# Rotary embedding on one half of each head: tile 2 loaded as 11 and 5 rows in place of 8 and 8

## The chip, the cores and the metric

The kernel runs on one core of a Trainium2 chip. The metric is the device time of one execution in microseconds. Before the change its median is 161.76 us over 3 runs (161.6 to 161.9).

## What is computed

The input `x` has the shape (16, 512, 16, 64) in float32: batch, sequence, heads, and 64 values per head. The tables `cos` and `sin` have the shape (512, 32). The first 32 values of each head are rotated; the other 32 are copied.

```
x1, x2 = x[..., :32], x[..., 32:]
c, s = cos[None, :, None, :], sin[None, :, None, :]
first  = x1[..., :16] * c[..., :16] - x1[..., 16:] * s[..., :16]
second = x1[..., :16] * s[..., :16] + x1[..., 16:] * c[..., :16]
out = concatenate([first, second, x2], axis=-1)
```

## The kernel before

Seen as one long array, `x` is cut into T = 4 tiles of 128 partitions. A partition holds K = 16 rows of the sequence, and a row is 16 heads of 64 values, 4 KB. A whole tile is 64 KB per partition, 8.4 MB in all. The tiles pass through SBUF in a ring of NS = 3 places (`ring`), tile t in place t modulo 3. Tiles are rotated in their place and stored from there, so tile 3 takes the place of tile 0 and can be loaded only when tile 0 has been stored.

`load` (L55) and `store` (L58) each issue one DMA over a stretch of rows, all loads and most stores from the queue of SP. SP works through its orders one by one: an order that waits holds up all orders behind it. Only the store of tile 2 is issued from GpSimd. SP's orders are, in this sequence: tile 0, tile 1, the upper 8 rows of tile 2 (`load(2, KC, K)`, KC = 8), the store of tile 0 (waits for VectorE), the lower 8 rows of tile 2, tile 3 (waits for the store of tile 0), the store of tile 1, the store of tile 3.

VectorE first builds the tables in all partitions (L61 to L83) out of two small loads that GpSimd issues (L63, L64). Then `rotate` does the work, four instructions per call over a stretch of rows of a tile: a product with sin into `b_t`, which lies in PSUM (L96), a product with cos in place (L97), a subtraction (L98) and an addition (L101). Tiles 0, 1 and 3 are rotated in two parts of 8 rows. Tile 2 is rotated as rows 8 to 15, rows 0 to 4 and rows 5 to 7; the border is KM = 5. The part with 5 rows is called `near`: a dependency written by hand (`tc.add_manual_dep`) lets the store of tile 1 wait until its last addition.

Of the kernel before, what the change touches and what calls it, by code (L numbers as in the profile page):

```python
# [1 line left out]

# [4 lines left out]


@with_exitstack
def kernel(  # L10
    ctx: ExitStack,
    tc: tile.TileContext,
    x: bass.AP,
    cos: bass.AP,
    sin: bass.AP,
    out: bass.AP,
):
    nc = tc.nc
    fp32 = mybir.dt.float32
    P = 128  # L20
    B, S, H, D = x.shape
    Q = D // 4
    HF = D // 2

    K = 16
    T = B * S // (P * K)
    PB = S // K
    REP = P // PB  # L30
    R = H * D
    NS = 3
    KC = K // 2
    KM = 5

    xf = x.rearrange("b s h d -> (b s h d)").rearrange("(t p f) -> t p f", t=T, p=P)
    of = out.rearrange("b s h d -> (b s h d)").rearrange("(t p f) -> t p f", t=T, p=P)
    cosf = cos.rearrange("(p k) j -> p (k j)", k=K)
    sinf = sin.rearrange("(p k) j -> p (k j)", k=K)

    const_pool = ctx.enter_context(tc.tile_pool(name="const", bufs=1))
    b_pool = ctx.enter_context(tc.tile_pool(name="bp", bufs=1, space=bass.MemoryType.PSUM))


    ring = const_pool.tile([P, NS, K, H, D], fp32)
    stage = const_pool.tile([P, 2, K, HF], fp32)
    spun = const_pool.tile([P, 2 * K, Q], fp32)
    packed = const_pool.tile([PB, 2 * K, Q], fp32)
    table = const_pool.tile([P, 2, K, 2, Q], fp32)

    def rows(t, lo, hi):
        return ring[:, t % NS, lo:hi].rearrange("p k h d -> p (k h d)")

    def load(t, lo=0, hi=K):
        return nc.sync.dma_start(out=rows(t, lo, hi), in_=xf[t, :, lo * R : hi * R])  # L55

    def store(t, lo=0, hi=K, queue=nc.sync):
        return queue.dma_start(out=of[t, :, lo * R : hi * R], in_=rows(t, lo, hi))  # L58


    nc.vector.memset(stage[:, :, :, 0:Q], 0.0)  # L61
    spread = stage.rearrange("(j b) t k i -> j b t (k i)", b=REP)
    nc.gpsimd.dma_start(out=spread[:, 0, 0], in_=cosf)  # L63
    nc.gpsimd.dma_start(out=spread[:, 0, 1], in_=sinf)  # L64
    load(0)
    load(1)
    load(2, KC, K)

    PQ = PB // REP
    nc.vector.stream_shuffle(  # L73
        out=spun[:],
        in_=stage.rearrange("p t k j -> p (t k) j")[:, :, 0:Q],
        mask=[j % PQ * REP for j in range(PB)],
    )
    for q in reversed(range(REP)):
        n = PQ * (q + 1)
        nc.vector.tensor_copy(out=packed[0:n], in_=spun[q * PB : q * PB + n])  # L80

    for r in range(REP):
        nc.vector.tensor_copy(  # L83
            out=table[r * PB : (r + 1) * PB].rearrange("p t k c j -> p (t k) c j"),
            in_=packed.unsqueeze(2).to_broadcast((PB, 2 * K, 2, Q)),
        )
    C = table[:, 0].rearrange("p k c j -> p k (c j)")
    Sn = table[:, 1].rearrange("p k c j -> p k (c j)")

    def rotate(t, lo, hi):  # L90
        x1 = ring[:, t % NS, lo:hi, :, 0:HF]
        c = C[:, lo:hi].unsqueeze(2).to_broadcast((P, hi - lo, H, HF))
        s = Sn[:, lo:hi].unsqueeze(2).to_broadcast((P, hi - lo, H, HF))
        b_full = b_pool.tile([P, KC, H, HF], fp32, name="b_t")
        b_t = b_full[:, 0 : hi - lo]
        nc.vector.tensor_mul(out=b_t, in0=x1, in1=s)  # L96
        nc.vector.tensor_mul(out=x1, in0=x1, in1=c)  # L97
        nc.vector.tensor_sub(  # L98
            out=x1[:, :, :, 0:Q], in0=x1[:, :, :, 0:Q], in1=b_t[:, :, :, Q:HF]
        )  # L100
        return nc.vector.tensor_add(  # L101
            out=x1[:, :, :, Q:HF], in0=x1[:, :, :, Q:HF], in1=b_t[:, :, :, 0:Q]
        )

    rotate(0, 0, KC)
    rotate(0, KC, K)
    store(0)
    load(2, 0, KC)
    load(3)
    rotate(1, 0, KC)  # L110
    rotate(1, KC, K)
    behind_loads = store(1)
    rotate(2, KC, K)
    near = rotate(2, 0, KM)
    rotate(2, KM, KC)
    store(2, queue=nc.gpsimd)

    tc.add_manual_dep(
        behind_loads.ins,
        near.ins.name,  # L120
        mybir.DependencyInfo(mybir.DependencyClass.Sync, mybir.DependencyReason.DATA),
        reason="the store follows the loads at the DMA engines",
    )
    rotate(3, 0, KC)
    rotate(3, KC, K)
    store(3)


# [1 line left out]
_INS = ['x', 'cos', 'sin']  # L130
_OUTS = [((16, 512, 16, 64), 'float32')]


# [23 lines left out]
```

## Time and profile before

| | |
|---|---|
| median of 3 runs | 161.76 us (161.6 to 161.9) |
| span of the profiled execution | 159.5 us |
| median less span | 2.3 us |
| VectorE busy | 112.9 us, 71% |
| DMA queues, share of 16 engines | 85.7% (SP's) and 12.4% (GpSimd's) |
| moved | 67.24 MB, 422 GB/s over the span |
| one rotation of 8 rows | 4.43 + 4.42 + 2.29 + 2.28 us on VectorE |
| store of tile 0 | issued at 49.92 us, lands after 21.8 us |
| load of tile 3 | issued at 71.72 us, lands after 29.0 us |
| last store | issued at 131.24 us, lands after 27.4 us |

Times in the trace are counted from the start of the span. A DMA order has two times: the issue on the queue's sequencer, some 0.4 us long, and the landing, when the last of the 16 DMA engines has reported. In between, the engines move packets, one for each partition and order, up to 64 KB long, eight of them per engine and order. The digits of the page's DMA line count a packet in the slice where it starts. The span begins and ends with the program's first and last instruction on the core; the run's time also holds what lies around it.

### The profile page before, as it was taken

To read this page: it belongs to the slowest core of one execution; us is meant where nothing else is said; L and a number is where in the kernel's file an instruction comes from. 1 tells how busy PE (TensorE), PEld (TensorE's weight loads), DVE (VectorE), ACT (ScalarE), POOL (GpSimd) and SP (SyncE) were. 2 spreads that over 40 slices of the span, in tenths; PEclk is the share of its full clock that TensorE was granted. 3 is DMA by queue.
4 is the path that set the end of the run, shared out by engine and by line. 5 is a ranking of instruction groups with operands and counts; after the bars stand their busy time and mean duration, and the time that the engine had idled before them with its cause. 6 is when DMAs were issued, how large, how long until landed. Compare 5 with 4: busy or idle time off the path is not lost.

```text
span 159.5 us, 115 instructions
## 1 busy us (share of the span) xinstructions
DVE 112.9 (71%) x47; POOL 1.9 (1%) x7
## 2 busy tenths in 40 slices
DVE  1000959999999999999999999999999990000000
POOL 3000000000000000000000000010000000000000
DMA  7969979799699699699996996996996997999966
GB/s 263 542 263 542 444 345 526 345 444 526 271 493 551 279 510 526 263 394 411 510 526 263 526 526 263 526 526 263 526 526 263 526 460 329 526 394 394 526 263 263
DMA packets 1360, 67.24 MB, mean 422 GB/s; under 512 B 176, under 2 KB 176, under 8 KB 208
## 3 DMA queue, kind: packets, MB, share of 16 engines
q1 hardware_dynamic: 1152, 58.72, 85.7%
q0 software_dynamic: 208, 8.52, 12.4%
HBM read 33.69 MB, written 33.55 MB: 422 GB/s over the span
## 4 chain that ended last, share of the span: by engine, by line
DVE 61%; DMA 14%; issue 5%; DVEq 1%
DVE b_t L96 22%; DVE ring L97 22%; DMA ring<-in_x_dram 14%; DVE ring L101 10%; DVE ring L98 7%; DVEq L152 1%; DVEq L96 0%
## 5 line engine op out<-in xcount | busy, mean ns | idle before, releaser
L96 DVE TENSOR_TENSOR b_t<-ring,table 128x4096 f32<-128x4096 f32 (+2 forms) x9 | 35.6, 3959 | 2.1 <-DMA ring<-in_x_dram 1.8
L97 DVE TENSOR_TENSOR ring<-ring,table 128x4096 f32<-128x4096 f32 (+2 forms) x9 | 35.5, 3950 | 0.3
L98 DVE TENSOR_TENSOR ring<-ring,b_t 128x2048 f32<-128x2048 f32 (+2 forms) x9 | 18.4, 2049 | 0.3
L101 DVE TENSOR_TENSOR ring<-ring,b_t 128x2048 f32<-128x2048 f32 (+2 forms) x9 | 18.4, 2043 | 0.0
L73 DVE LOAD_MASK_SELECT spun<-stage x1 | 0.0, 14 | 14.4 <-DMA stage<-in_sin_dram 14.4
L83 DVE COPY table<-packed 32x1024 f32<-32x1024 f32 x4 | 2.7, 684 | 0.1
L58 POOL DMA_DIRECT2D out_dram<-ring x1 | 0.6, 562 | 101.7 <-DVE ring L101 101.7
L80 DVE COPY packed<-spun 32x512 f32<-32x512 f32 (+3 forms) x4 | 1.7, 416 | 0.1
L61 DVE MEMSET stage<- 128x512 f32 x1 | 0.5, 485 | 0.9 <-PEq L141 0.9
L73 DVE STREAM_SHUFFLE spun<-stage 128x512 f32<-128x512 f32 x1 | 0.7, 721 | 0.0
L63 POOL DMA_DIRECT2D stage<-in_cos_dram x1 | 0.6, 644 | 1.3 <-DVE stage L61 1.3
L64 POOL DMA_DIRECT2D stage<-in_sin_dram x1 | 0.5, 535 | 0.0
L141 POOL MEMSET const-bfloat16-1.0<- 128x1 bf16 x1 | 0.1, 102 | 0.0
L141 POOL MEMSET const-float32-0.0<- 128x1 f32 x1 | 0.1, 99 | 0.2 <-issue 0.2
L141 POOL MEMSET const-float32-1.0<- 128x1 f32 x1 | 0.1, 99 | 0.0
L141 POOL MEMSET const-uint8-127<- 128x1 uint8 x1 | 0.1, 99 | 0.0
## 6 DMA issues: line engine op xcount, KB each, us to landing
ring<-in_x_dram SPq DMA_DIRECT2D x2, 4096.0 KB, 40.7
stage<-in_cos_dram POOLq DMA_DIRECT2D x1, 64.0 KB, 9.0
stage<-in_sin_dram POOLq DMA_DIRECT2D x1, 64.0 KB, 13.3
ring<-in_x_dram SPq DMA_DIRECT2D x3, 29.0
out_dram<-ring SPq DMA_DIRECT2D x3, 27.4
out_dram<-ring POOLq DMA_DIRECT2D x1, 39.5
```

The costliest lines, as they stand in the source:

```text
L58: return queue.dma_start(out=of[t, :, lo * R : hi * R], in_=rows(t, lo, hi))
L61: nc.vector.memset(stage[:, :, :, 0:Q], 0.0)
L63: nc.gpsimd.dma_start(out=spread[:, 0, 0], in_=cosf)
L64: nc.gpsimd.dma_start(out=spread[:, 0, 1], in_=sinf)
L73: nc.vector.stream_shuffle(out=spun[:], in_=stage.rearrange("p t k j -> p (t k) j")[:, :, 0:Q], mask=[j % PQ * REP for j in range(PB)],)
L80: nc.vector.tensor_copy(out=packed[0:n], in_=spun[q * PB : q * PB + n])
L83: nc.vector.tensor_copy(out=table[r * PB : (r + 1) * PB].rearrange("p t k c j -> p (t k) c j"), in_=packed.unsqueeze(2).to_broadcast((PB, ...
L96: nc.vector.tensor_mul(out=b_t, in0=x1, in1=s)
L97: nc.vector.tensor_mul(out=x1, in0=x1, in1=c)
L98: nc.vector.tensor_sub(out=x1[:, :, :, 0:Q], in0=x1[:, :, :, 0:Q], in1=b_t[:, :, :, Q:HF])
L101: return nc.vector.tensor_add(out=x1[:, :, :, Q:HF], in0=x1[:, :, :, Q:HF], in1=b_t[:, :, :, 0:Q])
L152: with _tile.TileContext(nc) as tc:
```

## The change

The rows of tile 2 are divided otherwise over its two loads. Ahead of the store of tile 0 SP now orders rows 5 to 15 (11 rows), and behind it rows 0 to 4 (5 rows). VectorE's parts of tile 2 become rows 8 to 15, rows 3 to 7 and rows 0 to 2. The store of tile 1 still waits for the part with 5 rows, which now holds rows of both loads. Nothing else changes, neither in the number of instructions nor in their order.

```diff
     KC = K // 2
-    KM = 5
+    KA = 5
+    KM = 3
...
     load(0)
     load(1)
-    load(2, KC, K)
+    load(2, KA, K)
...
     rotate(0, 0, KC)
     rotate(0, KC, K)
     store(0)
-    load(2, 0, KC)
+    load(2, 0, KA)
     load(3)
     rotate(1, 0, KC)
     rotate(1, KC, K)
     behind_loads = store(1)
     rotate(2, KC, K)
-    near = rotate(2, 0, KM)
-    rotate(2, KM, KC)
+    near = rotate(2, KM, KC)
+    rotate(2, 0, KM)
     store(2, queue=nc.gpsimd)
```

## The prediction

> **What bounds the kernel now.** I read the page first, for which resource is full.
>
> ```profile
> span 159.5 us, 115 instructions
> DVE 112.9 (71%) x47; POOL 1.9 (1%) x7
> DMA  7969979799699699699996996996996997999966
> DMA packets 1360, 67.24 MB, mean 422 GB/s; under 512 B 176, under 2 KB 176, under 8 KB 208
> q1 hardware_dynamic: 1152, 58.72, 85.7%
> q0 software_dynamic: 208, 8.52, 12.4%
> ```
>
> VectorE works 71% of the span. The packets of the two DMA queues fill 85.7 + 12.4 = 98.1% of what the 16 DMA engines have. The slices that read 6 beside slices that read 9 are no gaps: a packet is counted whole where it starts, and a 64 KB packet (2.4 us) is shorter than a slice (4 us), so slices hold one or two rounds of them. The packet records settle that: from 1.76 us to 158.2 us each of the 16 engines starts its next packet as the one before it ends; no gap is longer than 0.11 us.
>
> So the kernel is one unbroken transfer, and its end is a sum of packets. Per engine: 56 packets of 64 KB, 2.414 us from start to start (135.2 us); 16 of 32 KB, 1.2095 us each (19.4 us); the small packets of the two tables (0.3 us). The first packet starts at 1.76 us and takes 0.75 us more than the others, and where the first store hands over to a load some 0.35 us is lost. That makes 157.8 us; the last packet ends at 158.2, the last semaphore comes at 158.6, and the span is 159.5. The shown runs have a median of 161.76, so 2.3 us lie outside the span, and nothing in the change touches them.
>
> The chain of waits says otherwise, "DVE 61%; DMA 14%", because it walks back from the last store's issue and from there along VectorE. The last store is issued at 131.24 us, but the engines still have work of the two stores before it until 143.4 us: VectorE is not what ends last. I therefore go by the packets and not by that chain.
>
> Second, when the queue gets its orders, and when they land (the DMA sequencer's part of the timeline, stretches around two issues; then the DMA issues of the same stretches, whose last number is us from issue to landing; then the queue's own waits):
>
> ```profile
> 1.65 0.42 SPq L55 DMA_DIRECT2D ring<-in_x_dram  x1
> 49.92 0.35 SPq L58 DMA_DIRECT2D out_dram<-ring  x1
> 50.31 0.43 SPq L55 DMA_DIRECT2D ring<-in_x_dram  x1
> 71.72 0.33 SPq L55 DMA_DIRECT2D ring<-in_x_dram  x1
> ```
>
> ```profile
> ring<-in_x_dram SPq DMA_DIRECT2D x1, 4096.0 KB, 50.4
> ring<-in_x_dram SPq DMA_DIRECT2D x1, 4096.0 KB, 31.0
> ```
>
> ```profile
> SPq L55 <- DMA out_dram<-ring: 21.0, 1, 21.0
> SPq L58 <- DMA ring<-in_x_dram: 22.3, 2, 20.9
> ```
>
> The upper 8 rows of tile 2, issued at 1.65, land at 52.0. The store of tile 0, issued at 49.92, lands 21.8 us later, at 71.7. The lower 8 rows, issued at 50.31, land at 81.35. The load of tile 3 waits 21.0 us on SP for the store of tile 0, is issued at 71.72 and lands at 100.7. One queue, in order, without a break.
>
> Third, VectorE around the moved rows (timeline):
>
> ```profile
> 90.26 2.83 DVE L96 TENSOR_TENSOR b_t<-ring,table 128x2560 f32<-128x2560 f32 x1
> 98.90 0.34 SPq L58 DMA_DIRECT2D out_dram<-ring  x1
> 98.91 1.77 DVE L96 TENSOR_TENSOR b_t<-ring,table 128x1536 f32<-128x1536 f32 x1
> 104.36 4.43 DVE L96 TENSOR_TENSOR b_t<-ring,table 128x4096 f32<-128x4096 f32 x1
> ```
>
> It takes 8, then 5, then 3 rows of tile 2, and the end of the 5 releases the store of tile 1 at 98.90.
>
> **VectorE's parts.** The order on VectorE stays 8, 5, 3 rows with the same twelve instructions. Only which rows are meant changes: rows 3 to 7 and then 0 to 2, where it was 0 to 4 and then 5 to 7. The step that releases the store of tile 1 is again the end of the 5-row part: 2.83 + 2.82 + 1.49 + 1.48 us, issue at 98.90 as before. The sum is nothing. The first 8 rows, at 76.82, need the first load alone, now landing near 55.6: 21 us of cover. The 5-row part at 90.26 now reads from both loads; the later lands near 81.3, cover 8.9 us, and only beyond that would VectorE pay. Tile 3 is needed at 104.36 and lands at 100.7, cover 3.7 us; VectorE itself is 11 us early (131.24 plus 1 us to first data, against 143.4).
>
> **The loads.** No byte and no packet is added: 8 packets of 44 KB and 8 of 20 KB per engine stand for 16 of 32 KB. From 2.414 against 2 x 1.2095 us a packet has a fixed part of 0.005 us, so 44 KB takes 1.661 us and 20 KB 0.758 us; the pair is 2.419 us, as two of 1.2095 are. The trace has neither size; from below and above stand 32 KB and 64 KB at the same rate, for 20 KB only the 32 KB row. If each new packet were cut in two, 16 x 0.005 = 0.08 us would come on top; a gain has no row. I take 0.
>
> **The first store.** It is issued at the same 49.92 but has 3 rows more ahead of it: 8 x (1.661 - 1.2095) = 3.6 us. Its data start near 54.6 in place of 51.0, and it lands near 75.3 in place of 71.7. Behind it on SP stand the second load of tile 2, which waits for nothing and is issued at 50.31 as before, and the load of tile 3, which waits for this store: now about 75.3. Its cover is the second load, now 5 rows: 8 x 0.758 = 6.1 us of data from about 74.6 on, until 80.7. With 1.01 us from issue to first packet (first load: issue 0.74, packet 1.75) the order is ready at 76.3, 4.4 us ahead, where it was 8 us. If that cover were gone, each us of lateness would be a us of the end. After 80.9 everything is where it was. Sum: 0.
>
> **The seam at 51 us.** Before, the store's first packet starts 1.06 us after its issue, as the first engine runs dry: 0.04 us to spare against 1.01. The engine that runs dry last, at 51.6, has 0.66 us to spare, and that one sets the end. So there is no idle time to win in this execution, and a gain needs an execution with a later store. From the row the sum is 0; bounds: 0 to a gain of 0.3 us, the spread of the three runs (161.6 to 161.9), and on the other side the loss of the one seam with a long-queued order, next.
>
> The Trainium skill, "DMA: Bandwidth & Descriptors", Specifications, gives a first-byte latency of about 0.6 us for orders from this queue; the trace shows 1.01 us. By the page the first engine would have had 0.46 us to spare; the gain would be 0 by either, and the measured one leaves less room.
>
> **A seam that the trace does not show.** Before, both handovers from loads to a store (51 and 100 us) have the store's order arriving just in time, 1 us after its issue; in both nothing is lost (at most 0.04 us longer packets). Now the first store waits 4.7 us in the queue behind loads. The only handover with opposite directions and a long wait in the queue is the one from store to load at 71 us: the last 16 store packets took up to 3.33 us in place of 2.42, on average 0.35 more, and the last engine ended 0.33 us late. So the unseen seam costs between 0 (the seams of the same direction) and 0.33 us, with 0.91 us (the worst packet) as the far end; below nothing has no row. I take 0, the rows of the same direction. The seam at 71 us stays, with 20 KB packets behind it: its 0.33 us may move by some of itself, either way.
>
> **The rivals.** Slower: the early store disturbs the loads still ahead of it, as the load behind the first store disturbs that store's last packets. Place: the last 44 KB packets, 52 to 55 us. Price 0.33 to 0.91 us: 162.1 to 162.7, I say 162.2. It decides if those packets run over 1.661 us by 0.3 us on the engine that ends last. For it: this meeting is not in the trace, and its mirror costs. Against: loads queued behind loads, and stores queued behind a store, lose nothing.
>
> Faster: in executions without a profile the store comes too late for the seam at 51 us, and three rows more close the gap. Price up to 0.33 us beyond what can be seen: 161.4. For it: 0.04 us to spare on the first engine. Against: 0.66 us on the engine that ends last.
>
> The change that does nothing at all is my forecast itself: the same packets, in another order, on engines that never pause. A late load of tile 3 would be a further case; it has 4.4 us, so I give it no chance of its own.
>
> **How the numbers follow.** Forecast: 159.5 + 0 + 2.3, so 161.75, own range 161.45 to 162.05; chance 0.55. Slower rival 0.29, faster rival 0.16. A measurement of this kernel can tell about 0.2%, 0.32 us, from no change; the rivals' prices lie at or over that. The range that holds 8 in 10 reaches over most of both rivals: 161.35 to 162.6.
>
> **What would show it.** Right: the store of tile 0 issued at 49.9 and landing near 75.3; load of tile 3 issued near 75.3 and landing near 100.7; the stores of tiles 1 and 3 issued at 98.9 and 131.2; no gap at any engine. Slower rival: packets of 44 KB beyond 1.7 us just before the store, every later landing late by as much. Faster rival: same span, but lower times of runs. Wrong altogether: tile 3 landing after 104.4, VectorE waiting at 76.8 or 90.3, or 44 and 20 KB packets off the rate of 27 GB/s per engine.

## The result: 0.35% slower

The changed kernel has a median of 162.25 us over 5 runs (161.86 to 162.37); the kernel before had 161.6 us over 5 runs (161.27 to 161.9). The ratio is 1.0035, with a 95% interval of 1.0023 to 1.0048. The likeliest case of the prediction was no change, 161.75 us; what came is the rival that was called slower, with its 162.2 us.

A profile shows a single execution, not always a typical one; the changed kernel's is the shortest of its five, with 161.86 us. The page of the changed kernel first. VectorE and the bytes are the same to the digit, and only the span has grown by 0.6 us:

```profile
span 160.1 us, 115 instructions
DVE 112.9 (71%) x47; POOL 1.9 (1%) x7
DMA packets 1360, 67.24 MB, mean 420 GB/s; under 512 B 176, under 2 KB 176, under 8 KB 208
q1 hardware_dynamic: 1152, 58.72, 85.7%
q0 software_dynamic: 208, 8.52, 12.3%
```

The queues' share stays 98% although the span is longer, so the added time is inside packets: the engines hardly pause (no gap between two packets is longer than 0.18 us), and some packets last longer. Next SP's part of the timeline, the landings of the two loads of tile 2 (last number: us from issue to landing), and SP's wait for the store:

```profile
1.64 0.42 SPq L56 DMA_DIRECT2D ring<-in_x_dram  x1
50.06 0.35 SPq L59 DMA_DIRECT2D out_dram<-ring  x1
76.29 0.33 SPq L56 DMA_DIRECT2D ring<-in_x_dram  x1
```

```profile
ring<-in_x_dram SPq DMA_DIRECT2D x1, 5632.0 KB, 54.7
ring<-in_x_dram SPq DMA_DIRECT2D x1, 2560.0 KB, 31.5
```

```profile
SPq L56 <- DMA out_dram<-ring: 25.4, 1, 25.4
```

The 11 rows land at 56.4 us; 52.0 + 3.6 = 55.6 was forecast. The store of tile 0 lands at 76.3 (forecast 75.3), and the 5 rows at 81.9, where the 8 rows landed at 81.35. Tile 3 lands at 101.3 (100.7 before) and the last store at 159.2 (158.6). From the landing of tile 1 to that of the second load of tile 2 the kernel before needs 39.06 us, the changed one 39.50; from there to the last landing 77.26 and 77.28. So the loss lies between 42 and 82 us; the rest of the span's growth is the 0.14 us by which this execution was later at 42 us.

Where it lies can be seen in stretches set around the starts of packets: a row with share 0.00 is a stretch in which no packet starts (columns: stretch, its length, busy us of VectorE and GpSimd, clock, DMA share, GB/s; a packet counts whole where it starts). Changed kernel, the last two rounds of 44 KB packets, then the first of the store:

```profile
51.00:52.25 1.25, 1.25 (x1) 0.00 (x0) 1.00 1.35 577
52.25:53.25 1.00, 1.00 (x1) 0.00 (x0) 1.00 0.00 0
53.25:53.90 0.65, 0.65 (x1) 0.00 (x0) 1.00 3.57 1109
53.90:55.50 1.60, 1.56 (x2) 0.00 (x0) 1.00 0.00 0
55.50:56.10 0.60, 0.60 (x1) 0.00 (x0) 1.00 4.04 1748
```

The empty stretch between the rounds is 1.00 us long, and the one between the last round and the store 1.60. In the packet records the last 44 KB packets take 2.09 to 2.49 us and not 1.66, on average 0.65 us more. That is the seam which the trace of before could not show. Kernel before, the same seam: 0.50 us empty ahead of the last round and 0.50 behind it:

```profile
49.20:49.70 0.50, 0.50 (x1) 0.00 (x0) 1.00 0.00 0
49.70:50.40 0.70, 0.67 (x2) 0.00 (x0) 1.00 1.73 749
50.40:50.90 0.50, 0.50 (x1) 0.00 (x0) 1.00 0.00 0
```

The seam behind the store moved the other way. Kernel before, ahead of and in the store's last round, 1.75 and 2.15 us empty:

```profile
66.10:67.85 1.75, 1.72 (x2) 0.00 (x0) 1.00 0.00 0
67.85:68.55 0.70, 0.70 (x1) 0.00 (x0) 1.00 3.95 1498
68.55:70.70 2.15, 2.15 (x1) 0.00 (x0) 1.00 0.00 0
```

Changed kernel, the store's last round:

```profile
72.50:73.00 0.50, 0.50 (x1) 0.00 (x0) 1.00 4.53 1966
73.00:74.85 1.85, 1.85 (x2) 0.00 (x0) 1.00 0.00 0
```

Here no packet of that round is longer than 2.418 us; before, they lost 0.34 us on average and the next round 0.05. So the changed kernel pays 0.65 us at the first seam, 0.17 in earlier 44 KB packets (44 to 48 us), and saves some 0.37 at the second: 0.45 in sum. These are means over the engines; the mean landing of the second load came 0.54 us later (three more rounds of 44 KB packets lost 0.02 us each), the last one, on which the end hangs, the 0.44 us above.

### The profile page after: what moved, and what is told of

It reads as the page before. It is cut to its first block, busy times and chain, and to the rows that moved or that the text cites. A ratio compares the mean times of both kernels' runs of the same rounds, so it can differ in the third digit from the quotient of the medians.

```text
span 160.1 us, 115 instructions
## 1 busy us (share of the span) xinstructions
DVE 112.9 (71%) x47; POOL 1.9 (1%) x7
## 4 chain that ended last, share of the span: by engine, by line
DVE 61%; DMA 14%; issue 5%; DVEq 1%
DVE b_t L97 22%; DVE ring L98 22%; DMA ring<-in_x_dram 14%; DVE ring L102 10%; DVE ring L99 7%; DVEq L153 1%; DVEq L97 0%
```

## The experiments

Two theories stood at the start. **Theory 1, the waiting order**: a store whose order lies in the queue while loads ahead of it still run lengthens the last packets of those loads. **Theory 2, the rows**: long rows that begin inside a partition's 64 KB are slow by themselves. "Ready" is the issue plus 1.01 us. Each ratio is to the kernel before on the same chip, with its 95% interval. "Loss" is the mean over the 16 engines of what a round of packets takes over its size's usual time. "On the last engine" is another measure: by how much the latest end of a round moved beyond the usual time, counted from the latest end of the round before.

**The store held back in the changed kernel.**

```diff
-    store(0)
+    held = store(0)
...
-    rotate(1, 0, KC)
+    rotate(1, 0, KC, cut=6)      # first product of tile 1 as 6 and 2 rows
...
+    tc.add_manual_dep(held.ins, firsts[1, 0].ins.name, ...)   # the product over 6 rows
```

> The changed kernel, with the store of tile 0 held back until a product over 6 rows of tile 1 is done (the first product of tile 1 is cut into 6 and 2 rows), so that it is issued near 53.4 us and not at 50.06. Theory 1, the waiting order: the store costs 0.6 us because its order lies in the queue for 4.9 us behind loads; held back, the last 44 KB packets of the load take 1.66 to 1.7 us again (changed kernel: 2.09 to 2.49 us) and the time falls by 0.5 to 0.7 us, to that of the kernel before. Theory 2, the rows: 44 KB rows that begin 20 KB into a partition's 64 KB are slow by themselves; the last packets stay at 2.1 us and above and the time stays 0.35% over the kernel before.

Ratio 1.0085 (1.0071 to 1.0098). The first seam did as theory 1 says: no loss in the last 44 KB packets, 11 rows landed at 55.9. But the store's own last packets lost 0.32 us on average and 1.23 at worst, and the landings of the 5 rows lie 2.39 us apart between the first engine and the last (0.41 in the kernel before, 0.59 in the changed one). The mean engine finished the whole kernel as in the changed one (158.9 us both), the last at 160.7 and not 159.2. The end is the last engine's: the time that theory 1 forecast did not come, and since a new loss took the old one's place, this run does not tell what the first seam alone is worth. Its profiled execution took 163.62 us, where the median is 162.92.

**The store early in the kernel before.** The rotation of the upper half of tile 0 is left out, with three unread products in its place.

```diff
     rotate(0, 0, KC)
-    rotate(0, KC, K)
     store(0)
+    filler(0, 0, KC)             # three products into b_t
```

> The kernel before, loads of 8 and 8 rows, with the store of tile 0 issued early: the rotation of the upper 8 rows of tile 0 is left out and three products that nobody reads stand in its place behind the store, so VectorE's times stay within 0.2 us and the store is issued near 36.5 us, 14.5 us before the loads ahead of it end. Theory 1 (the waiting order): the last 32 KB packets ahead of the store take 0.4 to 0.8 us longer than 1.213 us, and the time rises by 0.5 to 0.7 us, 0.3 to 0.45%. Theory 2 (the rows): no 44 KB rows, so no change, within 0.2%.

Ratio 1.0044 (1.0032 to 1.0057). Sizes are untouched and the store is issued at 36.53 us. The last two rounds of 32 KB packets lost 0.34 and 0.77 us (stretches as above; the empty one behind the last round is 1.30 us, 0.50 before):

```profile
49.30:50.10 0.80, 0.77 (x2) 0.00 (x0) 1.00 0.00 0
50.10:50.80 0.70, 0.70 (x1) 0.00 (x0) 1.00 2.83 749
50.80:52.10 1.30, 1.30 (x1) 0.00 (x0) 1.00 0.00 0
```

Here too the second seam lost nothing. Theory 2 can't make this.

**The kernel before without its hand-written dependency.**

```diff
-    tc.add_manual_dep(behind_loads.ins, near.ins.name, ...)
```

> The kernel before without the hand-written dependency: the store of tile 1 is issued at 76.8 us and not at 98.9, some 23 us before the load of tile 3 ahead of it ends. Theory 1 (the waiting order): the last 64 KB packets of the load of tile 3 take 0.4 to 0.8 us longer than 2.418 us, tile 3 lands near 101.4 us and the time rises by 0.5 to 0.7 us. Theory 2 (the rows): no change, within 0.2%.

Ratio 1.0059 (1.0042 to 1.0075). The store of tile 1 was issued at 76.98 us, the first seam stayed free, and the last round of tile 3's 64 KB packets lost 1.24 us (2.90 us empty behind it, 1.80 ahead):

```profile
95.70:97.50 1.80, 1.77 (x2) 0.00 (x0) 1.00 0.00 0
97.50:98.10 0.60, 0.60 (x2) 0.00 (x0) 1.00 6.10 1748
98.10:101.00 2.90, 2.83 (x3) 0.00 (x0) 1.00 0.00 0
```

The loss follows the order that waits, to the other place, and here the store's order waits alone, with no load queued behind it. That dependency earns 0.6%. (The profiled execution took 163.0 us, the median is 162.37.)

**The load behind the first store held back.**

```diff
-    load(2, 0, KC)
+    late = load(2, 0, KC)
...
+    tc.add_manual_dep(late.ins, firsts[1, KC].ins.name, ...)  # first product of tile 1's upper half
```

> The kernel before, with the second load of tile 2 (behind the store of tile 0) held back until the first product of the upper half of tile 1 is done, issued near 67.84 us and not at 50.31, some 2.5 to 3 us ahead of the end of the store. Theory 1, taken for both directions (an order that waits long behind transfers of the other direction costs 0.3 to 0.6 us): the last packets of the store take 2.42 us again (before: up to 3.33 us) and the time falls by 0.3 to 0.4 us, 0.2 to 0.25%. Theory 1 for loads ahead of a store alone, and theory 2: no change; if the first packets of a load that comes just in time pay what the first load pays at the start (0.75 us), up to 0.4 us slower.

Ratio 1.001 (1.0001 to 1.002). Issued at 67.80, the load moved the loss but did not remove it: 0.06 us in the store's last round, then 0.15 and 0.23 in the first two rounds of the load, 0.44 for 0.39. Theory 1 does not hold for a load behind a store.

**Both kernels once more**, for second profiles.

> The changed kernel once more, for a second profile. If the seams behave the same each time: the last 44 KB packets ahead of the store of tile 0 take 0.6 to 0.7 us longer on the mean of the engines, the last packets of that store lose nothing (under 0.1 us), and the time is 0.3 to 0.4% over the kernel before. If the first profile's pattern was chance, the loss at the second seam comes back to the 0.34 us of the kernel before.

> The kernel before once more, for a second profile. If the seams behave the same each time: no loss in the last packets ahead of the store of tile 0, 0.3 to 0.6 us on the mean of the engines in the last packets of that store. Time: the same, within 0.2%.

Ratios 1.0037 (1.0024 to 1.0051) and 0.9997 (0.9984 to 1.001). Changed: 0.47 us at the first seam, under 0.03 at the second, 0.22 in the earlier 44 KB packets. Before: nothing, 0.34 and 0.05. From tile 1's landing to the second load's: 39.63 and 39.08 us. The pattern is the kernels', not chance.

**9 rows ahead and 7 behind.**

```diff
-    KA = 5
+    KA = 7
```

> The changed kernel with 9 rows ahead of the store of tile 0 and 7 behind it. The store's order then waits 1.2 us in the queue, between the 0 of the kernel before and the 3.6 us of the changed one. Theory 1, the loss grows with the wait: 0.2 to 0.3 us in the last 36 KB packets; time 0.1% over the kernel before. Theory 1b, any order that is there before the last packet starts costs the same: 0.5 us or more, time 0.3% over. Theory 2, the rows: loss in the packets that begin inside the partition's 64 KB, from 43 us on, and no more than 0.1 us at the last packet.

Ratio 1.0011 (1.0001 to 1.0021). Ready at 51.15, as the last 36 KB packets begin (51.15 to 51.94), the order cost nothing: no loss at the first seam, and 0.05 at the second. The second to fourth rounds of 36 KB packets lost 0.23 us together. Neither form of theory 1 as written held: a wait of 1.2 us is not a small part of the cost, it is free. (The profiled execution took 162.09 us, the median is 161.78.)

**The 11 rows as 3 and 8.**

```diff
-    load(2, KA, K)
+    load(2, KA, KC)
+    load(2, KC, K)
```

> The changed kernel with the 11 rows ahead of the store as two loads, rows 5 to 7 and then rows 8 to 15: the store's order waits as long as in the changed kernel, but no packet is 44 KB long; the last ones ahead of the store are the 32 KB packets of the kernel before. Theory 1 (the waiting order): the last 32 KB packets take 0.5 to 0.8 us longer, and the 0.19 us that the changed kernel lost in its 44 KB packets before the store was issued is gone; time 0.2 to 0.3% over the kernel before. Theory 2 (the rows): no loss, time that of the kernel before.

Ratio 1.007 (1.0044 to 1.0096). No 44 KB packets, and the last two rounds of 32 KB packets lost 0.24 and 0.66 us. Theory 2 is out as the cause of the first seam's loss. The time is more than was expected (0.2 to 0.3%), and the seven runs lie far apart, from 161.91 to 163.66 us; why, the profile of one of them does not show.

**10 rows ahead and 6 behind** (`KA = 6`).

> The changed kernel with 10 rows ahead of the store of tile 0 and 6 behind it. With 9 and 7 rows the order was ready near 51.15 us, as the last packets began, and nothing was lost at the seam; with 11 and 5 it was ready 2.2 us before they began and 0.5 to 0.65 us were lost. Here it is ready near 51.1 us, about 1.1 us before the last 40 KB packets begin. If the loss grows with the time that the order lies there before the last packet begins: 0.2 to 0.4 us, time 0.2 to 0.25% over the kernel before. If it is a step: 0.5 us or more, time 0.3% over; or still nothing, time 0.1% over.

Ratio 1.006 (1.0046 to 1.0073), the largest loss of the three splits. Ready near 50.85, the order came as the last round but one began (50.77 to 51.15), and that round lost 0.69 us, the last one 0.28 (empty stretches 1.70 and 1.20 us for rounds of 1.51 us less their spread):

```profile
50.75:51.15 0.40, 0.40 (x1) 0.00 (x0) 1.00 5.51 1638
51.15:52.85 1.70, 1.70 (x1) 0.00 (x0) 1.00 0.00 0
52.85:53.50 0.65, 0.65 (x1) 0.00 (x0) 1.00 2.76 1008
53.50:54.70 1.20, 1.17 (x2) 0.00 (x0) 1.00 0.00 0
```

So it does not grow evenly with the wait (9 rows: nothing, 10: 0.96, 11: 0.65 and 0.47). It is nearer to a step, between an order that comes as the last packets begin and one that comes a round earlier.

**9 rows as 1 and 8.** The edit of "three and eight" with `KA = 7`.

> 9 rows ahead of the store and 7 behind it, the 9 as two loads of 1 and 8 rows, so that no long row begins inside the partition's 64 KB but at its half. The run with 9 and 7 rows lost nothing at the first seam, 0.1 us at the second (kernel before: 0.4 us) and 0.23 us in its first 36 KB packets. If those 0.23 us come from the rows' length and place, they are gone here, the engines end 0.2 to 0.3 us earlier than in the kernel before, and the time is 0.1 to 0.2% under it. If they come from elsewhere: time 0.1% over the kernel before, as with 9 and 7.

Ratio 1.0007 (0.9985 to 1.0029). The 0.23 us of the 36 KB packets are gone and the seams lost 0.02 and 0.05 us, but 0.30 us on the last engine at the first; and the kernel is not faster than before. Its engines finish the second load 0.8 us apart (0.41 before), and the last needs 39.17 us for what took 39.06.

**The hold placed as with 9 rows** (`cut=4` in the first experiment's edit), twice.

> The changed kernel with the store of tile 0 held back until a product over 4 rows of tile 1 is done (6 rows in the earlier run), so that it is issued near 52.4 us and ready near 53.4, as the last 44 KB packets begin, the place at which the run with 9 and 7 rows lost nothing at either seam. If that place is what decides: last 44 KB packets 1.66 to 1.75 us, second seam under 0.15 us, no engine left behind, and the time 0.1% over the kernel before (the 0.2 us of the first 44 KB packets stay) instead of 0.35%. If the 11 and 5 rows are at fault whatever the store does: 0.35% over, or more, as in the earlier held run.

> The held kernel (11 and 5 rows, store of tile 0 issued near 52.3 us) once more, for a second profile and a second set of times. If the time that the profile lacks was chance: 0.1 to 0.25% over the kernel before. If it is there again: 0.3 to 0.4% over, with engines that land further apart than the 0.3 us of the kernel before at the end.

Issued at 52.25 and 52.35. The first seam lost 0.10 and 0.08 us, the second 0.04 us or less, and the mean engine came back to 81.0 and 81.1 us at the second load (81.1 before, 81.6 changed). The times came back by little: 1.0034 (1.0022 to 1.0046) and 1.0041 (1.0027 to 1.0055). The landings tell why the mean is no measure: the last engine needs 39.35 and 39.23 us from tile 1 to the second load, and at the end the engines land 0.58 and 0.66 us apart, in the kernel before 0.29. In both profiles the engine that began its last 44 KB packet last also lost the most in it, 0.27 and 0.26 us, so that on the last engine the first seam still costs half of what it costs in the changed kernel (0.54 and 0.56 us; in the kernel before 0.00). The stretches of the first of these profiles, the last 44 KB packets and the store behind them, look free, but they do not show the last of the 16 engines, which begins its first packet of the store only at 55.62:

```profile
53.15:53.75 0.60, 0.60 (x1) 0.00 (x0) 1.00 2.94 1201
53.75:54.85 1.10, 1.07 (x2) 0.00 (x0) 1.00 0.00 0
54.85:55.60 0.75, 0.75 (x1) 0.00 (x0) 1.00 3.03 1311
```

**Tile 0 as 15 rows and 1 row**, in the kernel before.

```diff
-    load(0)
+    load(0, 0, K - 1)
+    load(0, K - 1, K)
```

> The kernel before, with tile 0 loaded as 15 rows and 1 row, so that VectorE begins some 1.2 us earlier (it needs the first 8 rows alone) and the store of tile 0 is issued near 48.7 us, ready near 49.75, as the last 32 KB packets ahead of it begin, and not as they end. If an order that comes there saves the loss at the second seam, as with 9 and 7 rows: nothing lost at the first seam, under 0.1 us at the second (kernel before: 0.39 us), every landing behind it 0.3 us earlier, time 0.2% under the kernel before. If the second seam's loss has another cause, or the order is there too early: the same time, or 0.2 to 0.4% over.

Ratio 1.0072 (1.0051 to 1.0093). The store was issued at 49.10 and both seams were free on average (0.07 us in two rounds, and 0.02). But tile 1 already landed 0.42 us later than in the kernel before, the last engine lost 0.59 us in those two rounds, and the engines land 1.3 us apart at the second load. A seam that is free on average is worth nothing if the engines drift apart.

**The hold without 44 KB packets** (held back as above, 11 rows as 3 and 8).

> The held kernel with the 11 rows ahead of the store as loads of 3 and 8 rows: no 44 KB packets, and the store's order near 52.3 us, which is now 1.1 us before the last 32 KB packets begin (near 53.5 us). If the rest of the held kernel's time is the rows' (0.1 to 0.2 us in the first 44 KB packets): those are gone, but the order is there before the last packets begin, as with 10 and 6 rows, and 0.3 to 0.9 us are lost in the last two rounds of packets: 0.3 to 0.6% over. If 1.1 us of waiting ahead of the last packet are still free: 0.1% over or less.

Ratio 1.0045 (1.0031 to 1.0058). The last round lost 0.15 us, the order being ready 0.3 us ahead of it: mostly free again on average, but not on the last engine, which lost 0.41 us. The time stays, so the rows' length is not what keeps the held kernels slow.

**The cut alone**, in both kernels: the first product of tile 1 as 4 and 4 rows, nothing held.

> The kernel before with the first product of tile 1 cut into 4 and 4 rows and nothing held back. VectorE is 0.17 us later from there on, and the store of tile 1 is issued near 99.1 us, 0.2 us after the last engine-free margin of the kernel before (ready at 100.1, first engine free near 99.9, last near 100.3). If the cut costs nothing: within 0.1% of the kernel before. If it is what keeps the held kernels slow: 0.2 to 0.35% over.

> The changed kernel with the same cut and nothing held back: the store of tile 0 is issued near 50.06 us and waits behind the loads. If the hold gained what the profile says and the cut took it back: 0.5 to 0.7% over the kernel before, against 0.34 to 0.41% with the hold. If the cut is free and the hold gained nothing: 0.35%, as the changed kernel.

Ratios 1.0004 (0.9995 to 1.0012) and 1.0053 (1.0036 to 1.0070). The cut is free in the kernel before. The changed kernel with the cut lost 0.28 us at the first seam and 0.34 in earlier 44 KB packets; against it the hold gains 0.1 to 0.2%, and the intervals overlap.

## Why the prediction was right and wrong

**Right: the bound.** The engines hardly pause, and the sum over packets explains the end. The landing times show 0.44 us more on the way to the second load, the timed runs 0.57 (0.0035 x 161.6).

**Right: VectorE and the loads behind.** The releases came at 99.04 and 131.38 us, 0.14 us behind those of before, as the first load landed 0.14 us later. The load of tile 3 was issued at 76.29, and its cover held (the 5 rows still ran until 81.9).

**Wrong: the seam that the trace does not show.** The prediction named it, priced it from its mirror at 0.33 to 0.91 us, and took 0, "the rows of the same direction". It measured 0.65 and 0.47 us on average (0.54 and 0.56 on the last engine), 0.28 with the cut. Loads behind loads were no nearer row than the mirror: what they lack is the change of direction, and the one row that had it was not free. The rival's place (the last 44 KB packets), price and point of decision (0.3 us on the last engine; its packet took 2.20 us, 0.54 over) were right, its chance too small. That its 162.2 us met the measured 162.25 so closely is luck in part: it had one term, and the runs show three, a loss at this seam, a smaller one ahead of it and a gain behind it.

**Wrong: both handovers from loads to a store were read as free.** They are free as long as the order comes within the last packet: with these two orders brought forward, the same handovers lost 1.11 and 1.24 us. "Just in time" was taken there as a margin that could only be lost on the late side; for the early side the forecast took the low end of its bounds, nothing.

**Missed: the second seam.** It was expected to stay; its 0.39 us (0.33 on the last engine) went away wherever the first store's order was ready about a packet's time or more before the loads ran out, and was 0.3 us or more in every run where it came later. That is why the change costs less than its first seam.

**Sized at nothing, measured above it:** the new packets. They have the rate forecast (1.662 and 0.761 us at the shortest), but 0.14 to 0.34 us were lost in rounds of 44 KB packets before the store was even issued (0.17 and 0.22 in the two profiles of the changed kernel), and 0.23 with 36 KB; with 40 KB none. Why, no run shows.

**Misread, without effect:** VectorE was not 11 us early for the last store. The last packet of the store of tile 2 ends at 141.3 us, but a round of the last store's packets, begun at 136.2, already lies ahead of it. Without that round the engines would run dry near 138.7, some 6.4 us after the last store's order is ready (an estimate from these packet times). The changed kernel used up 0.14 us of it.

The Trainium skill, "DMA: Bandwidth & Descriptors", Specifications, gives a first-byte latency of about 0.6 us for orders from this queue. By an estimate from that figure the store of the run with 9 and 7 rows would be ready 0.4 us ahead of the last packets; with the 1.01 us of the trace it is ready as they begin.

**What stays open.** That an early order lengthens the last packets ahead of it and costs time is shown by two runs without any new row (1.0044, 1.0059). That taking it away brings the changed kernel back is not: held back, the first seam is all but free for the mean engine, and 0.34 to 0.45% stay. Part of that shows on the last engine, which still loses 0.26 to 0.41 us at the first seam in the runs held with `cut=4`; up to the second load it is 0.29 and 0.17 us behind the kernel before in two of them, where the timed runs are 0.55 and 0.66 us behind. The cut is not the cause, nor are the 44 KB packets. Why an order that is ready as the last packets begin still costs the last engine that much with 11 and 5 rows, and nothing with 9 and 7 (1.0011; 0.30 us with the 9 as 1 and 8), was not tried by itself, and that the late engines are what the timed runs pay is argued from the packets and landings only. Why an early order lengthens the last packets, and spares the next seam, no run shows; the same page says, under "Two DMAs through the same engine are not ordered", that an engine's read and write sides are separate queues, which might let the store's reads run beside the last loads; no record here separates the two sides. No version was faster than the kernel before.

## What to carry to other kernels

Where the DMA engines are full, a queue should not go dry, but an order of the other direction need not lie in it long before its turn either: here a store issued 1 to 2.4 us before the first engine ran out of loads cost nothing at the seam in the kernel before and with 9 and 7 rows, and the two kernels in which a store's order was brought forward, by 13 and 22 us, and no row changed were 0.44 and 0.59% slower. A row that stands for an unseen case must share what makes the case new; where one row has it and others do not, the price is that row's. And with 16 engines in step, look at the landing of the last one beside the mean: a loss that falls on the engines ahead costs less than its size (in the last packets of the first store up to 0.91 us in the kernel before, and the end of the round moved by 0.33), one that falls on the last is paid in full.

## What was not expected of the hardware

- The loss at a handover from loads to a store is, on the mean of the engines, near a step: 0.15 us or less with the order ready no more than 0.3 us before the last packets begin, 0.28 to 0.96 us with it ready a round earlier or more, 1.11 us at 13 us and 1.24 us at 20 us ahead of the last packets. On the last engine it is less of a step: nothing to 0.41 us of the last round in the first case, 0.42 us and more in the others.
- The handover from a store to loads costs 0.39 us on average in the kernel before, whether the load waits 20 us or 3 us in the queue, and under 0.1 us where the store itself had come early.
- One engine alone can fall behind by 2 us and stay there: in the profile of the first held run, one execution, the landings were 0.58 us apart at tile 1 and 2.4 us apart at the second load, and still 2.2 us apart at the end.
